# Queries, keys and all gates of a hybrid attention block as Strassen units

## The chip, the core and the metric

The kernel runs on one core of a Trainium2 chip. The core has a matrix engine (TensorE, PE in the profile; its loads of the stationary operand are the row PEld), three engines for elementwise work (VectorE or DVE, ScalarE or ACT, GpSimd or POOL) and SyncE (SP), whose queue issues all transfers of this kernel. The metric is the device time of one execution in microseconds. Before the change the median of three runs is 2264.71 us (2264.17 to 2265.93).

## What is computed

One block of a decoder for 1024 tokens of width 1024, in float32. From one normalised input come, through one wide projection, the queries, keys and values of 12 attention heads of 128, the queries, keys (256 wide), values (512) and output gates of 4 retention heads, and two gates of width 1024:

```python
xn = rmsnorm(x, norm1_g[l])
qa, ka, va, qr, kr, vr, gr, gate_a, gate_b = [xn @ wl[:, bounds[i]:bounds[i + 1]] for i in range(len(IN_SPLITS))]
qa = rmsnorm(qa.reshape(B, S, ATT_HEADS, ATT_HEAD_DIM), q_norm_g[l])
ka = rmsnorm(ka.reshape(B, S, ATT_HEADS, ATT_HEAD_DIM), k_norm_g[l])
...
y = jax.nn.sigmoid(gate_a) * (o_a @ w_proj_a[l]) + jax.nn.sigmoid(gate_b) * (o_r @ w_proj_b[l])
x = x + y @ w_out[l]
```

`o_a` is causal sliding-window attention in three groups of four heads with dilations 1, 4 and 16, whose outputs are mixed by their softmax denominators; `o_r` is chunkwise retention with a group norm and a swish gate. A squared-ReLU MLP follows, which the change does not touch.

## The kernel before

All large products are float32 split in two: a high part rounded to the matrix engine's fast format (`wh`, `xh`), and the rest (`wl`, `xl`). Each product of two blocks is three matmuls (high by high, high by low, low by high), issued by `Pipe.group` (L223). `split` (L319 on ScalarE, L320 on VectorE) makes the two parts. `Weights` loads raw weights through SP (L176) and splits them when the buffer that they go to has been freed by the last product that reads it.

TensorE's order is that of the program text; the other engines' instructions are ordered by a scheduler. `Pipe` counts one slot for each large product (`step`) and lets other work be laid between its terms: `pipe.at(lag, fn)` puts `fn` into the product `lag` slots on, spread evenly over its terms.

The part that the change touches has three stages.

Attention: for each head and each of 8 blocks of 128 tokens, one product gives q, k and v of that head (tokens on partitions, 384 columns, 24 matmuls). q and k are squared and normalised with tokens on partitions (L650, L332, L333, L654), a pair of transposes (`turn_qk`, L660) puts features on partitions, and ScalarE and VectorE write them out in the order of the dilation (L662, L664). Scores (L584), the turn of the probabilities (L597) and their product with the values (L604) are laid into later products of the stage. The groups' outputs go to DRAM and are mixed (`load_heads`, `combine`, `turn_mixed`) while the next heads run, the last ones during retention.

Gates: the first 3 of 8 pairs of gate blocks are plain products of 512 columns, with the sums and differences of the input blocks (`differences`) made alongside.

Strassen units: a unit is a product of 256 output features with all 1024 inputs and tokens, done as seven products (N1 to N7) of 12 matmuls of 512 columns instead of eight, features on partitions. `strassen_order` sets their order, `product` runs one and evicts it: N2 gives one of the four results straight from PSUM, N3 one from `u2` (copied at N6, then a subtraction on VectorE, L402), N7 one from `u3` (a copy on ScalarE, L396, then a subtraction, L397), N4 one from PSUM. `W.free` then lets the next weights into the buffer. Units are 5 gate pairs, 8 retention q and k, and 8 output gates of retention.

Of the kernel before, what the change touches and what calls it, by code (L numbers as in the profile page):

```python
# [17 lines left out]
P = 128  # L18
S = 1024
# [237 lines left out]
def strassen_order(units):  # L257
# [12 lines left out]
def hybrid_block(ctx: ExitStack, tc: tile.TileContext, a: dict, out: bass.AP):  # L270
# [13 lines left out]
    tr = ctx.enter_context(tc.tile_pool(name="tr", bufs=2, space=PSUM))  # L284
    ms = ctx.enter_context(tc.tile_pool(name="ms", bufs=3, space=PSUM))
# [9 lines left out]
    v_d = dram.tile([HEADS, S, DH], F, name="v_d")  # L295

# [25 lines left out]
    half = const.tile([P, 2], F, name="half")  # L322
# [5 lines left out]
    const.tile([P, 224], F, name="rest")  # L328
# [12 lines left out]
    for slot, g in heads:  # L341
        for u in range(4):
            W.add(a["w_att"][g * SLOTS + slot, u])
    for d, bufs in enumerate([(0, 1), (2, 4), (3, 5)]):
        for u, b in enumerate(bufs):
            W.add(a["w_gate"][d, u], b)
    NG, NQ = KT - 3, 2 * RH
    W.add_units("in", [a["w_gate_q"][j] for j in range(NG)] + [a["w_rqk_q"][j] for j in range(NQ)]
                + [a["w_gr_q"][j] for j in range(8)])
# [68 lines left out]
    def dilated(g, b, src, dst):  # L418

        if g == 0:  # L420
            return src, dst[:, b * P:(b + 1) * P]
        r = 4 if g == 1 else 8
        src = src.rearrange("p (i r) -> p r i", r=r)
        if g == 1:
            nb, j = divmod(b, 4)
            return src, dst.rearrange("p (r i) -> p r i", r=r)[:, :, nb * P + 32 * j:nb * P + 32 * j + 32]
        return src, dst.rearrange("p (r i) -> p r i", r=r)[:, :, 16 * b:16 * b + 16]
# [62 lines left out]
    attn = ExitStack()  # L490
    p3 = pool(attn, "p3", 2, "right")
    p2 = pool(attn, "p2", 2, "right")
    cpa = pool(attn, "cpa", 1, "right")
    with ExitStack() as ph:
        cp = pool(ph, "cp", 1)
        first = ExitStack()
        px = pool(first, "px", 2)
        cmb = None

        g1 = cp.tile([P, D], F, name="g1")  # L500
        gq = cpa.tile([P, HEADS], F, name="gq")
        gk = cpa.tile([P, HEADS], F, name="gk")
        dist = cp.tile([P, 2, 2 * P], F, name="dist")
# [55 lines left out]
        pipe.at(0, lambda: W.pump())  # L559
        nc.sync.dma_start(gq, a["q_norm_g"])  # L560
        nc.sync.dma_start(gk, a["k_norm_g"])
        nc.sync.dma_start(dist, a["c_dist"])

        for head, (slot, g) in enumerate(heads):
            h = g * SLOTS + slot
            slope = 2.0 ** (-8.0 * (h + 1) / HEADS)
            us = W.take(4)
            bias = p2.tile([P, 2 * P], F, name="bias")
            qT = p2.tile([P, S], F, name="qT")
            kT = p2.tile([P, S], F, name="kT")  # L570
            V = p2.tile([P, NT, DH], F, name="V")
            Vd = p2.tile([P, NT, DH], F, name="Vd") if g > 0 else V
            acc = p2.tile([P, NT, DH + 2], F, name="acc")

            def attend(g, h, b, bias, qT, kT, V, acc):

                nk = 2 if has_prev(g, b) else 1
                n = nk * P
                k0 = (b + 1 - nk) * P
                st = {}  # L580

                def scores():
                    sp = ms.tile([P, 512], F, name="ms")
                    nc.tensor.matmul(sp[:, :n], qT[:, b * P:(b + 1) * P], kT[:, k0:k0 + n], start=True, stop=True)  # L584
                    s = p3.tile([P, 2 * P], F, name="s")
                    mx = p3.tile([P, 1], F, name="mx")
                    nc.vector.tensor_tensor_reduce(s[:, :n], sp[:, :n], bias[:, 2 * P - n:], op0=OP.add, op1=OP.max,
                                                   scale=1.0, scalar=-3.0e38, accum_out=mx)
                    nc.vector.tensor_scalar(acc[:, b, DH:DH + 1], mx, -1.0, None, op0=OP.mult)
                    st["p"] = p3.tile([P, 2 * P], F, name="pr")  # L590
                    nc.scalar.activation(st["p"][:, :n], s[:, :n], AF.Exp, bias=acc[:, b, DH:DH + 1],
                                         accum_out=acc[:, b, DH + 1:DH + 2])

                def turn():
                    tp = ms.tile([P, 512], F, name="ms")
                    for j in range(nk):
                        nc.tensor.transpose(tp[:, j * P:(j + 1) * P], st["p"][:, j * P:(j + 1) * P], ident)  # L597
                    st["t"] = p3.tile([P, 2 * P], F, name="pT")
                    nc.vector.tensor_copy(st["t"][:, :n], tp[:, :n])

                def values():
                    po = ms.tile([P, 512], F, name="ms")
                    for j in range(nk):
                        nc.tensor.matmul(po[:, :DH], st["t"][:, j * P:(j + 1) * P], V[:, k0 // P + j, :],  # L604
                                         start=(j == 0), stop=(j == nk - 1))
                    nc.scalar.activation(acc[:, b, :DH], po[:, :DH], AF.Copy)
                    if b == NT - 1:
                        store()

                def store():  # L610
# [9 lines left out]
                return scores, turn, values  # L620

            for b in range(NT):
                if b == 1:
                    nc.vector.tensor_scalar(bias, dist[:, 0 if g < 2 else 1, :], -slope * (DIL[g] if g < 2 else 8),
                                            None, op0=OP.mult)
                if head == 0 and b + 2 < NT:
                    norm1(b + 2)
                if head == 1 and b == 4:
                    first.close()
                    cmb = pool(ph, "cmb", 2)  # L630
                if head >= 3:
                    i = head % 3
                    if i < 2 and b == 6:
                        at = load_heads(head // 3 - 1, i, cmb)
                    if i > 0 and b == 1:
                        mixing = combine(head // 3 - 1, i - 1, cmb, at)
                    mix_next()
                if head == 0 and b == 1:
                    nc.vector.tensor_scalar(gq, gq, DH ** -0.5, None, op0=OP.mult)
                ts = slice(b * P, (b + 1) * P)  # L640
                pm = mm.tile([P, 512], F, name="mm")
                o = [(k % 2) * 384 for k in range(KT)]
                w = [W[us[k // 2]] for k in range(KT)]
                ends = {2 * i + 1: (lambda i=i: W.free(us[i])) for i in range(4)} if b == NT - 1 else None
                pipe.step(pm[:, :384], [(*X(k, ts), w[k][0][:, o[k]:o[k] + 384],
                                         w[k][1][:, o[k]:o[k] + 384]) for k in range(KT)], ends)
                ss = p3.tile([P, 4], F, name="ssa")
                junk = p3.tile([P, P], F, name="junk")
                for j in range(2):
                    nc.scalar.activation(junk, pm[:, j * DH:(j + 1) * DH], AF.Square, accum_out=ss[:, j:j + 1])  # L650
                rsqrt(ss[:, 2:4], ss[:, 0:2], 1.0 / DH)
                qk = p3.tile([P, 2, DH], F, name="qk", bufs=3)
                nc.scalar.activation(V[:, b, :], pm[:, 2 * DH:3 * DH], AF.Copy)
                nc.vector.tensor_tensor(qk, pm[:, :2 * DH].rearrange("p (a d) -> p a d", a=2),  # L654
                                        ss[:, 2:4, None].to_broadcast([P, 2, DH]), op=OP.mult)

                def turn_qk(g=g, b=b, h=h, qk=qk, qT=qT, kT=kT):
                    pt = tr.tile([P, 4, P], F, name="tr")
                    for j in range(2):
                        nc.tensor.transpose(pt[:, j, :], qk[:, j, :], ident)  # L660
                    src, dst = dilated(g, b, pt[:, 0, :], qT)
                    nc.scalar.activation(dst, src, AF.Copy, scale=gq[:, h:h + 1])  # L662
                    src, dst = dilated(g, b, pt[:, 1, :], kT)
                    nc.vector.tensor_scalar(dst, src, gk[:, h:h + 1], None, op0=OP.mult)  # L664
# [698 lines left out]
```

## Time and profile before

| | before |
|---|---|
| median of three runs | 2264.71 us |
| profiled execution, its time | 2268.99 us |
| its span, first to last instruction | 2267.2 us |
| TensorE busy, share of the span | 2233.0 us, 98% |
| VectorE, ScalarE, GpSimd busy | 1285.7, 1014.0, 344.3 us |
| attention, first product to first gate product | 10.64 to 521.84 us |
| gates and units, up to retention | 521.84 to about 1001 us |
| mean granted TensorE clock | 0.998 |
| moved by transfers | 294.85 MB, 130 GB/s |

In a row of the order of time stand the start in us, the length in us, the engine, the line, the operation, output and inputs, shapes and a count. Matmuls overlap in the pipeline, so the length of one is longer than the distance to the next. In the grouped rows stand busy time and mean nanoseconds of one, then the idle time of the engine before them. A row of the waits reads: engine, output and line, what it waited for, total us, times, longest.

### The profile page before, as it was taken

The numbers are of one execution on the slowest core, as the hardware profiler recorded it, in microseconds if no ns is written. First come the engines' busy times: TensorE is split into PE (matmuls) and PEld (weight loads), VectorE is DVE, ScalarE is ACT, GpSimd is POOL, SyncE is SP. The second block draws the span as 40 slices with busy tenths as digits, with TensorE's granted clock in tenths as the row PEclk, the third lists the DMA queues.
The fourth block names the chain that finished last, engine by engine and source line by source line (L and its number), as shares of the span: only waits on it lengthen the run. The fifth ranks groups of instructions, "written<-read, shape, count | busy, mean of one in ns | idle before, by whom it ended". The sixth has DMA issues, their size and how long they took to land. (4 is left out here: it accounts for less than half of the span.)

```text
span 2267.2 us, 30458 instructions
## 1 busy us (share of the span) xinstructions
PE 2233.0 (98%) x10868; PEld 1912.0 (84%) x10868; DVE 1285.7 (57%) x2468; ACT 1014.0 (45%) x2294; POOL 344.3 (15%) x372
## 2 busy tenths in 40 slices
PE   8999999999999999999999999999999999899999
PEld 7999999998888888888888878888788888788777
DVE  6444545455544445558676753253855556687874
ACT  5444434345433333345555633112555545654542
POOL 1111111110000000000000000000000000587873
PEclk9999999999999999999999999999999999999999
DMA  4313232323233333363433385554345556645432
GB/s 148 98 52 105 65 91 85 94 85 99 82 109 106 110 109 111 113 186 117 122 117 97 121 267 183 155 184 153 107 127 151 151 152 199 218 153 179 169 129 102
DMA packets 227146, 294.85 MB, mean 130 GB/s; under 512 B 14129, under 2 KB 157873, under 8 KB 226994
## 3 DMA queue, kind: packets, MB, share of 16 engines
q1 hardware_dynamic: 226994, 292.91, 41.1%
q8 instruction: 85, 1.39, 0.3%
q14 instruction: 67, 0.55, 0.1%
HBM read 200.48 MB, written 92.37 MB: 129 GB/s over the span
## 5 line engine op out<-in xcount | busy, mean ns | idle before, releaser
L320 DVE TENSOR_TENSOR wl<-raw,wh 128x1024 fp32r<-128x1024 f32 (+2 forms) x274 | 300.4, 1099 | 398.0 <-ACT wh L319 396.9
L223 PE MATMUL mm<-wh,xh 128*128 128x384 f32 (+1 forms) x1226 | 482.0, 393 | 0.6 <-DVE Y L1203 0.5
L223 PE MATMUL mm<-wh,xl 128*128 128x384 f32 (+1 forms) x1226 | 438.8, 358 | 2.2 <-DVE xl L320 2.2
L223 PE MATMUL mm<-wl,xh 128*128 128x384 f32 (+1 forms) x1226 | 437.7, 357 | 0.0
L319 ACT ACTIVATE wh<-raw 128x1024 fp32r<-128x1024 f32 (+2 forms) x274 | 260.0, 951 | 358.2 <-PE ms L223 102.2
L223 PE MATMUL mm<-xl,wh 128*128 128x512 f32 x848 | 309.3, 389 | 1.7 <-DVE xl L320 1.7
L223 PE MATMUL mm<-xh,wh 128*128 128x512 f32 x848 | 309.7, 390 | 0.9 <-ACT ms L388 0.9
L223 PE MATMUL mm<-xh,wl 128*128 128x512 f32 x720 | 280.1, 389 | 0.0
L223 PEld LDWEIGHTS mm<-wh,xl 128*128 128x128 f32 x1226 | 230.9, 188 | 22.2 <-DVE xl L320 3.0
L223 PEld LDWEIGHTS mm<-wh,xh 128*128 128x128 f32 x1226 | 231.8, 189 | 20.0 <-DVE Y L1203 1.3
L223 PEld LDWEIGHTS mm<-wl,xh 128*128 128x128 f32 x1226 | 232.7, 190 | 16.6
L223 PE MATMUL ms<-xh,wh 128*128 128x512 f32 x604 | 239.3, 396 | 5.0 <-DVE s L941 3.5
L223 PE MATMUL ms<-xl,wh 128*128 128x512 f32 x604 | 235.8, 390 | 0.7 <-DVE xl L320 0.7
L223 PE MATMUL ms<-xh,wl 128*128 128x512 f32 x604 | 235.9, 391 | 0.0
L223 PEld LDWEIGHTS mm<-xl,wh 128*128 128x128 f32 x848 | 159.2, 188 | 34.9 <-DVE xl L320 2.1
L223 PEld LDWEIGHTS mm<-xh,wh 128*128 128x128 f32 x848 | 159.2, 188 | 34.2 <-ACT ms L388 1.3
L223 PEld LDWEIGHTS mm<-xh,wl 128*128 128x128 f32 x720 | 135.1, 188 | 28.1
L853 POOL TENSOR_TENSOR st<-st,half 128x1 f32<-128x1 f32 x32 | 25.8, 808 | 765.3 <-DVE st L852 765.3
L223 PEld LDWEIGHTS ms<-xh,wh 128*128 128x128 f32 x604 | 113.9, 189 | 31.2 <-issue 2.3
L223 PEld LDWEIGHTS ms<-xh,wl 128*128 128x128 f32 x604 | 113.7, 188 | 23.9
L223 PEld LDWEIGHTS ms<-xl,wh 128*128 128x128 f32 x604 | 113.9, 189 | 23.5 <-DVE xl L320 1.0
L333 POOL TENSOR_TENSOR ssa<-ssa,half 128x2 f32<-128x2 f32 x96 | 66.5, 693 | 427.9 <-DVE ssa L332 411.2
(296 smaller groups left out, 3605.1 us busy)
## 6 DMA issues: line engine op xcount, KB each, us to landing
raw<-in_w_att SPq DMA_DIRECT2D x48, 384.0 KB, 3.9
raw<-in_w_up SPq DMA_DIRECT2D x32, 512.0 KB, 3.9
h_d<-s SPq DMA_DIRECT2D x64, 256.0 KB, 4.5
raw<-in_w_down SPq DMA_DIRECT2D x32, 512.0 KB, 4.1
xh<-h_d SPq DMA_DIRECT2D x11, 896.0 KB, 4.5
xl<-h_d SPq DMA_DIRECT2D x10, 896.0 KB, 4.6
r<-h_d SPq DMA_DIRECT2D x10, 896.0 KB, 5.6
sg_d<-sg SPq DMA_DIRECT2D x32, 256.0 KB, 2.0
```

The source lines that it names most:

```text
L223: self.nc.tensor.matmul(ps, x, y, start=start, stop=stop, skip_group_check=not first)
L319: nc.scalar.activation(dst_h, src, AF.Copy)
L320: nc.vector.tensor_tensor(dst_l, src, dst_h.bitcast(F), op=OP.subtract)
L333: nc.gpsimd.tensor_tensor(dst, dst, half[:, :w], op=OP.pow)
L853: nc.gpsimd.tensor_tensor(st[:, 9:10], st[:, 8:9], half[:, 0:1], op=OP.pow)
```

## The change

The values of all heads become plain products ahead of everything, four heads at once (512 columns, 24 products of 24 matmuls), written to DRAM. The q and k of each head become one Strassen unit, and all 8 gate pairs become units. The units number 36 instead of 21, in a new order in which the next unit starts one unit ahead instead of two. With features on partitions no transposes of q and k are needed. The sum of squares over features then runs across partitions: a matmul with the squares as stationary operand and a column of ones. Norms are raised on GpSimd, turned, written to DRAM and read back broadcast over partitions; q and k go through DRAM as well, and a head's attention starts when its pieces have been read back and multiplied. Attention of a head takes 11 slots, 8 of them with scores, laid between unit products from the 24th slot on; all mixing follows after the last head, so none is left for retention. The N4 operand takes the place of one input block, which is kept in DRAM and read back at the end. `u2` and `u3` get one buffer instead of two; three PSUM buffers instead of two serve the inserted work, two instead of three the `ms` tiles.

```diff
+    if near:
+        order = [(0, "N1"), (0, "N2")]
+        for j in range(units):
+            for d, name in ((0, "N6"), (0, "N5"), (1, "N1"), (0, "N7"), (1, "N2"), (0, "N3"), (0, "N4")):
+                if j + d < units:
+                    order.append((j + d, name))
+        return order
...
-    tr = ctx.enter_context(tc.tile_pool(name="tr", bufs=2, space=PSUM))
-    ms = ctx.enter_context(tc.tile_pool(name="ms", bufs=3, space=PSUM))
+    banks = ExitStack()
+    tr = banks.enter_context(tc.tile_pool(name="tr0", bufs=3, space=PSUM))
+    ms = banks.enter_context(tc.tile_pool(name="ms0", bufs=2, space=PSUM))
...
-    NG, NQ = KT - 3, 2 * RH
+    NG, NQ, NH = KT, 2 * RH, HEADS
...
+        def head_piece(i, f, cs, src):
...
+            sq = ap.tile([P, 512], F, name="sq")
+            nc.scalar.activation(sq, src, AF.Square)
+            sg = src
+            if src.space == PSUM:
+                sg = sgp.tile([P, 512], F, name="sg")
+                nc.scalar.activation(sg, src, AF.Copy)
+            nc.sync.dma_start(qk_d[h, f, :, cs], sg)
...
+            def sums():
+                ps = tr.tile([P, 512], F, name="tr")
+                for c in range(4):
+                    nc.tensor.matmul(ps[:, c:c + 1], sq[:, c * P:(c + 1) * P], one, start=True, stop=True)
+                nc.vector.tensor_scalar(rs[:, f, t:t + 4], ps[:, :4], 1.0 / DH, EPS, op0=OP.mult, op1=OP.add)
+                norms[i][1] += 1
+                if norms[i][1] == 4:
+                    flat = rs.rearrange("p f t -> p (f t)")
+                    nc.gpsimd.tensor_tensor(flat, flat, half, op=OP.pow)
+                    pipe.at(2, turn_norms)
...
+            pipe.at(0, sums)
...
+        def norm_piece(i, n):
...
+            dst, raw, rb = dilated(g, hf, state[i]["qk"[f]], raw, rb)
+            nc.vector.scalar_tensor_tensor(dst, raw, (gk if f else gq)[:, h:h + 1], rb, op0=OP.mult, op1=OP.mult)
+
+        def open_head(i):
...
+            for n in range(4):
+                norm_piece(i, n)
+                if n < 2:
+                    load_piece(i, n + 2)
...
+            pipe.at(0, scores)
+            pipe.at(2, turn)
+            pipe.at(3, values)
+
+        PACE = NT + 3
+        starts = [pipe.slot + 24 + PACE * i for i in range(HEADS)]
...
-                pm = mm.tile([P, 512], F, name="mm")
-                o = [(k % 2) * 384 for k in range(KT)]
...
-                        nc.tensor.transpose(pt[:, j, :], qk[:, j, :], ident)
...
-        for j, name in strassen_order(NIN):
+        for j, name in strassen_order(NIN, near=True):
+            between()
```

How the instructions stand now is set by these tables and by the scheduler. First TensorE, in a product of the attention stage before (`mm` of 384 columns, a score matmul L584 and the pair of transposes L660 laid in):

```order
L584 MATMUL ms_2703<-kT_1675,qT_1674 128x256
L223 MATMUL mm_2679<-wh4_2531,xh_93 128x384
L223 MATMUL mm_2679<-wl4_2532,xh_93 128x384
L223 MATMUL mm_2679<-wh4_2531,xl_94 128x384
L223 MATMUL mm_2679<-wh5_2547,xh_93 128x384
L223 MATMUL mm_2679<-wl5_2548,xh_93 128x384
L223 MATMUL mm_2679<-wh5_2547,xl_94 128x384
L660 MATMUL tr_2717<-ident_101,qk_2596 128x128 x2
```

The pair stands behind the last but one term of a product of 24 matmuls. Now the product N2 of a unit, which follows N7 of the unit before; L754 are the values, L743 the turn, L653 the four sums over N7's squares, L730 the scores:

```order
L754 MATMUL tr_1883<-V0_1735,pT_1850 128x128
L223 MATMUL mm_1815<-xh_96,wh0_1521 128x512
L223 MATMUL mm_1815<-xl_97,wh0_1521 128x512
L223 MATMUL mm_1815<-xh_96,wl0_1522 128x512
L743 MATMUL tr_1889<-ident_104,pr_1832 128x128 x2
L223 MATMUL mm_1815<-xh_96,wh0_1521 128x512
L223 MATMUL mm_1815<-xl_97,wh0_1521 128x512
L223 MATMUL mm_1815<-xh_96,wl0_1522 128x512
L653 MATMUL tr_1897<-one_1211,sq_1868 128x1 x4
L223 MATMUL mm_1815<-xh_96,wh0_1521 128x512
L223 MATMUL mm_1815<-xl_97,wh0_1521 128x512
L223 MATMUL mm_1815<-xh_96,wl0_1522 128x512
```

The transposes are gone; the sums stand behind the ninth of the twelve matmuls of N2. Second, ScalarE around the end of N7, in a unit before (`wh5` is the split of weights that N7 frees, `u3` the copy of N7's result):

```order
L319 ACTIVATE wh5_7805<-raw0_7561 128x1024
L396 ACTIVATE u3_7801<-ms_7539 128x512
L750 ACTIVATE sg_7829<-mm_7774 128x512
L319 ACTIVATE wh4_6606<-raw2_7685 128x512
L750 ACTIVATE sg_7844<-ms_7539 128x512
```

And now (L642 are the squares, L737 the exponentials, L756 the copies of the attention's output):

```order
L330 ACTIVATE wh5_1871<-raw0_1493 128x1024
L737 ACTIVATE pr_1857,md_1699<-pr_1857,md_1699 128x128
L404 ACTIVATE u3_1865<-ms_1640 128x512
L756 ACTIVATE acc_1882<-tr_1883 128x128
L642 ACTIVATE sq_1868<-u3_1865 128x512
L330 ACTIVATE wh0_1919<-raw1_1877 128x1024
L642 ACTIVATE sq_1914<-mm_1815 128x512
L646 ACTIVATE sg_1916<-mm_1815 128x512
```

The split still goes ahead of the copy; the square of `u3` and the square of the next N2 are new, with work of attention between. Third, VectorE at the same place now:

```order
L734 ISA pr_1857,mx_1858<-tr_1855,bias_1698 128x128
L734 ISA mx_1858 128x1
L736 TENSOR_SCALAR md_1699<-mx_1858 128x1
L331 TENSOR_TENSOR wl5_1872<-raw0_1493,wh5_1871 128x1024
L405 TENSOR_TENSOR u3_1865<-u3_1865,mm_1792 128x512
L745 COPY pT_1892<-tr_1889 128x256
L654 TENSOR_SCALAR rs_1686<-tr_1897 128x4
```

The subtraction from `u3` stands behind the low half of the split, and the reading of the sums (L654) behind both.

More of the change, by code (lines that the diff above doesn't have):

```diff
@@ L560, in hybrid_block @@
+    with ExitStack() as ph:
+        pu = pool(ph, "pu0", 1)
+        attn = ExitStack()
+        ap = pool(attn, "ap", 2)
+        gq = ap.tile([P, HEADS], F, name="gq", bufs=1)
+        gk = ap.tile([P, HEADS], F, name="gk", bufs=1)
         nc.sync.dma_start(gq, a["q_norm_g"])
         nc.sync.dma_start(gk, a["k_norm_g"])
-        nc.sync.dma_start(dist, a["c_dist"])
-        for head, (slot, g) in enumerate(heads):
-            h = g * SLOTS + slot
[L566 to L610, printed above, removed]
@@ L618, in store @@
                         nc.sync.dma_start(acc_d[:, h, :].rearrange("(p r) e -> p r e", r=8), acc)
[L620 to L640, printed above, removed]
-                pm = mm.tile([P, 512], F, name="mm")
-                o = [(k % 2) * 384 for k in range(KT)]
[L643 to L664, printed above, removed]
-                s1, s2, s3 = attend(g, h, b, bias, qT, kT, Vd, acc)
-                lag = 2 if g == 0 else 9
-                pipe.at(lag + 2, s3)
-                pipe.at(lag + 1, s2)
-                pipe.at(lag, s1)
-                pipe.at(1, turn_qk)
@@ new lines, in hybrid_block, with between @@
+        mixes = starts[-1] + PACE + 4
+        cmb, at = None, {}
+        def between():
+            nonlocal mixing, cmb
+            now = pipe.slot
+            for i, start in enumerate(starts):
+                if now == start - 6:
+                    load_piece(i, 0)
+                    load_piece(i, 1)
+                if now == start - 3:
+                    open_head(i)
+                if now == start - 2:
+                    load_values(i, 0)
+                if now == start + 1:
+                    load_values(i, 1)
+                if start <= now < start + NT:
+                    attend(i, now - start)
+            if now == mixes - 1:
+                attn.close()
+                cmb = pool(ph, "cmb", 2)
+            n, m = divmod(now - mixes, 9)
+            if 0 <= n < 2 * SLOTS and m == 0:
+                at[n] = load_heads(n // 2, n % 2, cmb)
+            n, m = divmod(now - mixes - 5, 9)
+            if 0 <= n < 2 * SLOTS and m == 0:
+                mixing = combine(n // 2, n % 2, cmb, at[n])
+            mix_next()
@@ L770, in hybrid_block @@
                 start = values(first, slice(0, P), False)
+            if (j, name) == (NIN - 1, "N4"):
+                for i in range(2):
+                    nc.sync.dma_start(XS[0, 1][i].bitcast(F), x_d[i])
+        assert not mixing and not any(f >= pipe.slot for f in pipe.due), (pipe.slot, mixes, pipe.due.keys())
         W.more = None
     gst.close()
+    banks.close()
+    tr = ctx.enter_context(tc.tile_pool(name="tr", bufs=2, space=PSUM))
+    ms = ctx.enter_context(tc.tile_pool(name="ms", bufs=3, space=PSUM))
     ret = ExitStack()
@@ L1296, in _constants @@
     far = np.where((d >= 0) & (d <= P) & (k >= P) & (d % 2 == 0), d, BIG)
-    dist = np.stack([near, far], 1).astype(np.float32)
+    bias = []
+    for h in range(HEADS):
+        g = h // SLOTS
+        scale = -(2.0 ** (-8.0 * (h + 1) / HEADS)) * (DIL[g] if g < 2 else 8)
+        bias.append((near if g < 2 else far).astype(np.float32) * np.float32(scale))
     mask = np.zeros((P, RH, P), np.float64)
```

281 lines of the change are left out of this document (174 added, 107 removed).

## The prediction

> **What bounds the kernel now.** I read the busy times first, then what TensorE waited for, then its order of time. The page and the two lists of TensorE's waits (the first 530 us, then up to 996 us, which is the end of the part that the change rewrites):
>
> ```profile
> span 2267.2 us, 30458 instructions
> PE 2233.0 (98%) x10868; PEld 1912.0 (84%) x10868; DVE 1285.7 (57%) x2468; ACT 1014.0 (45%) x2294; POOL 344.3 (15%) x372
> ...
> PE mm L223 <- DVE xl L320: 2.2, 2, 1.7
> PE ms L584 <- DVE pT L599: 0.9, 1, 0.9
> ...
> PE ms L597 <- ACT sg L689: 0.4, 1, 0.4
> PE ms L604 <- ACT sg L689: 0.2, 1, 0.2
> ```
>
> After its first matmul TensorE waits under 5 us in this whole part. So the part lasts as long as TensorE has instructions for, and the change is priced in TensorE's time; whatever VectorE, ScalarE and the transfers do costs only where TensorE has to wait for it. The profiled execution took 2268.99 us, 1.8 us more than its span; the median of the runs is 2264.71 us, and I subtract from that, since a difference of instructions is the same in both.
>
> A busy figure of matmuls overlaps (390 ns each), so I take start-to-start times from the order of time:
>
> ```profile
> 299.81 0.33 PE L223 MATMUL mm<-wh,xh 128*128 128x384 f32 x1
> ...
> 302.75 0.34 PE L223 MATMUL mm<-wh,xl 128*128 128x384 f32 x1
> 302.94 0.38 PE L660 MATMUL tr<-ident,qk 128*128 128x128 f32 x2
> 303.07 0.42 PE L223 MATMUL mm<-wh,xh 128*128 128x384 f32 x1
> 303.33 0.34 PE L223 MATMUL mm<-wl,xh 128*128 128x384 f32 x1
> ...
> 991.80 0.39 PE L223 MATMUL mm<-wh,xl 128*128 128x512 f32 x1
> 997.92 0.39 PE L223 MATMUL ms<-xh,wl 128*128 128x512 f32 x1
> ```
>
> From 299.81 to 302.75 are 17 steps of 384 columns: 0.173 us each. From 991.80 to 997.92 are 27 steps of 512 columns: 0.2267 us. The pair of transposes stretches two steps from 0.346 to 0.58 us, so it costs 0.234 us.
>
> **Products: removed and added.** The attention projections are 12 heads x 8 blocks x 8 k x 3 = 2304 matmuls of 384 columns: 398.6 us. The three plain gate groups are 3 x 4 x 8 x 3 = 288 of 512: 65.3 us. The transposes of q and k, 96 pairs: 22.5 us. Removed: 486.4 us. Added: values plain, 3 x 8 x 8 x 3 = 576 of 512; 12 units of q and k and 3 more gate units, each 7 products of 12: 1260 of 512. That is 1836 x 0.2267 = 416.2 us. Scores, turns of the probabilities, values and the mixing are moved, with the same count. Net so far: -70.2 us.
>
> **The column of ones.** Each of 48 results (12 heads, q and k, two halves) now passes through four matmuls of one column whose stationary operand is a 128x128 float32 block of squares. No such matmul is in the trace. The nearest rows are the four passes of a float32 product with 128 columns (two products; the profile shows two passes for each), and the weight loads around such insertions:
>
> ```profile
> 525.71 0.40 PE L223 MATMUL ms<-xh,wl 128*128 128x512 f32 x1
> 525.94 0.61 PE L604 MATMUL ms<-V,pT 128*128 128x128 f32 x4
> 526.30 0.47 PE L223 MATMUL ms<-xh,wh 128*128 128x512 f32 x1
> 526.62 0.39 PE L223 MATMUL ms<-xl,wh 128*128 128x512 f32 x1
> ...
> 511.83 0.58 PEld L604 LDWEIGHTS ms<-V,pT 128*128 128x128 f32 x4
> ...
> 515.74 0.19 PEld L223 LDWEIGHTS mm<-wh,xh 128*128 128x128 f32 x1
> 515.85 0.19 PEld L223 LDWEIGHTS mm<-wl,xh 128*128 128x128 f32 x1
> ```
>
> The four passes cost 0.91 - 0.453 = 0.457 us, 0.114 each. With one column almost nothing streams, so the weight load must set the pace. Loads follow each other at 0.11 us where no long matmul lies between (515.74, 515.85), and at (0.58 - 0.19) / 3 = 0.13 within the four. Four matmuls make eight passes: 8 x 0.114 = 0.91 us, and 48 of these 43.8 us. Bounds: if half of each load ran under the one before, 22 us; if each took its whole 0.19 us, 8 x 0.19 x 48 = 73 us. I take 43.8, since the load spacing is the row closest to it.
>
> The Trainium skill ("TensorE: Matmul & The Clock Gate", section "Back-to-back issue gap") prices an isolated matmul of 1 to 64 columns at an issue floor of about 25 ns; by that the eight passes would take 0.2 us, 48 of them an estimated 10 us, and the kernel 34 us less than I say. The load spacing of 0.11 us speaks against it here, since every pass loads its own weights.
>
> Turning the 16 norms of a head costs half a pair of transposes, 12 x 0.117 = 1.4 us. The sums themselves are read by VectorE and raised on GpSimd, both of which have room: VectorE was busy 250 of 511 us in the attention part and 184 of 401 in the unit part:
>
> ```profile
> 10.64:521.84 511.20, 507.88 (x3137) 496.14 (x3136) 250.17 (x892) 235.58 (x927) 69.86 (x102) 1.00 0.29 88
> ...
> 595.00:996.00 401.00, 401.00 (x1770) 331.78 (x1769) 184.43 (x229) 147.53 (x212) 0.00 (x0) 1.00 0.34 112
> ```
>
> Squares on ScalarE (48 x 0.63) and the four multiplications of a head on VectorE (0.68 each, as the 512-wide L867) replace the 192 squares with their accumulators, the 96 qk multiplications and the 192 scaled evictions. They cost nothing as long as no product of TensorE waits. Without that cover each would cost its own length.
>
> Net without waits: -70.2 + 43.8 + 1.4 = -25.0 us.
>
> **The new waits.** The sums stand in the very next product, after nine of its twelve matmuls in most slots (the order of TensorE in the part on the change): 9 x 0.2267 = 2.04 us, plus the values and the turn ahead of them (0.35 to 0.69), so about 2.5 us after the product ends. Three of the four results make that. N2 and N4 are squared straight from PSUM behind one weight split (0.97 + 0.63 = 1.6 us). N3 needs a VectorE subtraction first (0.16 + 0.68 + 0.63 = 1.5 us). N7 does not. The same chain in the trace of before, where N7 of a unit ended and the next product started at 731.36:
>
> ```profile
> 731.36 0.39 PE L223 MATMUL mm<-xh,wh 128*128 128x512 f32 x1
> ...
> 731.33 1.06 ACT L319 ACTIVATE wh<-raw 128x1024 fp32r<-128x1024 f32 x1 [1.38 <-PE ms L223]
> 732.30 0.58 ACT L396 ACTIVATE u<-ms 128x512 f32<-128x512 f32 x1
> ...
> 732.43 1.23 DVE L320 TENSOR_TENSOR wl<-raw,wh 128x1024 fp32r<-128x1024 f32 x1 [1.70 <-ACT wh L319]
> 733.57 0.68 DVE L397 TENSOR_TENSOR u<-u,mm 128x512 f32<-128x512 f32 x1
> ...
> L746 ACT ACTIVATE sg<-u 128x512 f32<-128x512 f32 x13 | 8.2, 632 | 20.2 <-DVE u L402 12.7 <-DVE u L397 7.5
> ```
>
> The split of the freed weights goes ahead of the copy on ScalarE and ahead of the subtraction on VectorE, so the difference is ready 734.25 - 731.36 = 2.9 us after the product; a square of 0.63 us (as the sigmoid in L746) puts it at 3.5. The new order keeps both splits ahead, so TensorE would wait 3.5 - 2.5 = 1.0 us. Where the slot has no scores, the sums stand at the product's end and the next split (1.06 us) goes ahead of the square: 0.16 + 0.97 + 0.63 = 1.8 us. With three such slots in eleven the mean is 1.2 us, and 12 heads give 14.4 us. Behind the waiting sums stand the product's last matmuls, the scores and all later products: nothing of it is made up, since TensorE is the bound.
>
> Opening a head makes VectorE wait for two 256 KB loads that SP issues only after its first two multiplications:
>
> ```profile
> s<-sg_d SPq DMA_DIRECT2D x32, 256.0 KB, 3.3
> rqk_d<-u SPq DMA_DIRECT2D x16, 256.0 KB, 3.8
> ```
>
> From the last scores of the head before: about 4 us to the first two multiplications, 0.7 for two issues, 3.3 to land, 0.7 for the last: 9 us. The new head's scores are due four products later, 4 x 2.72 plus insertions, about 14: covered. But the copy of the last turned block stands behind it on VectorE, done at about 9.4 and due at about 10. I charge 0.4 us a head, 5 us (0 to 25). The store of u2, now in one buffer, lands about 0.9 + 0.35 + 3.8 = 5 us after N3, and the next u2 copy comes at 5.4 or later: nothing, and 4 us more of cover before N7. At the start the 2.2 us wait for xl shrinks, as the first products are a third longer: -1 us.
>
> Sum: -25.0 + 14.4 + 5 - 1 = -6.6 us, 2258.1 us.
>
> **Rivals.** (a) The waits stay hidden, or the one-column passes are cheaper than their loads suggest. For it: TensorE waited almost nowhere in either old part, and a square put ahead of the split would be in time. Against it: the order has the split ahead. No waits: 2264.7 - 26 = 2239; with passes at half a load too, 2217.
> (b) Slower: all four sums of a unit wait, not N7's alone. ScalarE then has the splits, the evictions, the squares and the exponentials of attention in one strict order, and each square is late by whatever stands ahead. For it: the margins of the other three are only 0.9 us, while one exponential takes 0.4 to 0.5 and one split 1.06. Against it: both engines were about half idle. If the other 36 sums wait x on average, the time is 2258.1 + 36x; it is slower than before by the measurable amount from x = 0.31 us. At x = 0.7 it is 2283.
> (c) Loads of float32 squares cost their whole 0.19 us: 73 instead of 43.8 us, 2287.
>
> **How the numbers follow.** This kernel's runs tell about 0.2% from no change, 4.5 us: below 2260.2 is faster, above 2269.2 slower. My case, 0.42, with a range of its own from 2248 to 2268: within it 0.25 faster, 0.13 same, 0.04 slower. Rival (a) 0.25, all faster. Rivals (b) 0.24 and (c) 0.09: 0.02 the same, the rest slower. That makes 0.50 faster, 0.15 same, 0.35 slower. The range takes in (a) with hidden waits and (b) and (c) at their prices: 2234 to 2287.
>
> **What would show it.** The matmuls L653 should hold their product up by 0.9 us per four (half of that: (a); 1.5: (c)). The list of TensorE's waits should show the first of L653 waiting for ScalarE's square of u3 a dozen times, near 1.2 us. If the squares of mm, u2 and ms stand there too, it is (b). The copies pT should show a few short waits near the opening of heads; the unit products should still start every 0.2267 us. The prediction is wrong if a wait that I took as covered, the loads at a head's opening above all, comes to several us for each head.

## The result and the profile after

The changed kernel takes 2303.49 us (median of four runs, 2296.13 to 2309.46), the kernel before 2265.32 us beside it: 1.0164 times as long, with a 95% interval of 1.0133 to 1.0196. It is slower by 38 us; 2258 us was predicted, with 2287 as the upper end of the range. The head of the page of the changed kernel's profiled execution:

```profile
span 2302.3 us, 29056 instructions
...
PE 2236.7 (97%) x10316; PEld 1834.5 (80%) x10316; DVE 1341.6 (58%) x2385; ACT 1034.6 (45%) x1910; POOL 315.1 (14%) x288
```

TensorE shows 552 matmuls fewer than before (10868), and the span is 35.1 us longer. The rewritten part holds the loss: the first matmul of retention starts at 1046.51 us instead of 1002.91, 43.6 us later, and what follows it is 8.5 us shorter than before. TensorE's waits in this part, of which there had been less than 5 us (us in total, times, longest):

```profile
PE tr L653 <- ACT sq L642: 15.6, 12, 2.0
PE tr L481 <- DVE oa L475: 10.2, 7, 4.0
PE tr L754 <- DVE pT L745: 4.8, 5, 1.9
...
PE mm L223 <- DVE u L405: 3.3, 4, 1.3
...
PE mm L223 <- ACT ms L396: 1.4, 1, 1.4
PE tr L663 <- POOL rs L658: 1.3, 1, 1.3
```

The first row is the one that was predicted: twelve waits of the sums (L653) for the square of N7. The second was not: the transposes of a mixed block (L481) wait for VectorE's mixing. The rows together have 36.6 us. And there is a cost that no list of waits shows. The table by stretches (from and to, length, busy time of PE, PEld, DVE, ACT and POOL with their counts, then the granted TensorE clock, the DMA share and GB/s):

```profile
150.00:450.00 300.00, 280.73 (x1409) 231.51 (x1407) 140.93 (x310) 117.23 (x248) 28.71 (x9) 0.95 0.42 130
450.00:840.00 390.00, 382.21 (x1870) 314.32 (x1869) 222.06 (x521) 185.84 (x378) 9.84 (x3) 1.00 0.53 154
840.00:1000.00 160.00, 149.32 (x634) 119.87 (x633) 102.48 (x236) 72.90 (x103) 0.00 (x0) 0.96 0.42 131
```

The clock was 0.95 in the stage of q and k, and 0.96 in the stage of the mixing: 0.05 x 300 + 0.04 x 160 = 21 us of TensorE's time. Over slices of 30 us, where the rounding matters less, it is 20.7 us. The kernel before had 1.00 there.

How the two belong together is seen in the order of time around the first N7 (start, length, engine, line, operation, and in brackets the idle time before it and what ended it):

```profile
172.52 0.58 ACT L404 ACTIVATE u<-ms 128x512 f32<-128x512 f32 x1
172.65 1.23 DVE L331 TENSOR_TENSOR wl<-raw,wh 128x1024 fp32r<-128x1024 f32 x1 [6.28 <-ACT wh L330]
...
173.79 0.68 DVE L405 TENSOR_TENSOR u<-u,mm 128x512 f32<-128x512 f32 x1
...
174.51 0.63 ACT L642 ACTIVATE sq<-u 128x512 f32<-128x512 f32 x1 [1.40 <-DVE u L405]
175.19 1.05 PE L653 MATMUL tr<-one,sq 128*128 128x1 f32 x8 [1.46 <-ACT sq L642]
176.10 0.48 PE L223 MATMUL mm<-xh,wh 128*128 128x512 f32 x1
...
177.61 0.63 PE L223 MATMUL mm<-xh,wh 128*128 128x512 f32 x1
...
178.03 0.63 PE L223 MATMUL mm<-xl,wh 128*128 128x512 f32 x1
...
178.46 0.63 PE L223 MATMUL mm<-xh,wl 128*128 128x512 f32 x1
```

The copy of N7 is there early; the subtraction stands behind a weight split of 1.23 us on VectorE, the square behind the subtraction, and TensorE waits 1.46 us. About 2.4 us after it works again, its matmuls start every 0.42 us instead of every 0.23, until the next sums at 180.17: half the clock. (The trace also records the granted clock with its times: 0.5 from 177.52 us, for 3.41 us.) So the wait is paid once as a wait, and a second time afterwards.

The mixing, later on:

```profile
898.70 0.49 PE L481 MATMUL tr<-ident,oa 128*128 128x128 f32 x3
...
900.96 1.23 DVE L331 TENSOR_TENSOR wl<-raw,wh 128x1024 fp32r<-128x1024 f32 x1 [1.12 <-ACT wh L330]
...
902.42 0.74 DVE L475 SCALAR_TENSOR_TENSOR oa<-at,w,oa 128x128 f32<-128x128 f32 x2
...
903.22 0.47 PE L481 MATMUL tr<-ident,oa 128*128 128x128 f32 x1 [4.03 <-DVE oa L475]
...
904.34 0.63 PE L223 MATMUL mm<-xh,wl 128*128 128x512 f32 x1
904.77 0.63 PE L223 MATMUL mm<-xh,wh 128*128 128x512 f32 x1
```

Three of the four transposes run; the fourth needs the last mixing step, which stands on VectorE behind the sums and splits of the weights for the next units. They are due one product after that step, and a product of a unit gives VectorE only 2.72 us. TensorE waits 4.03 us, and half the clock follows.

The theory to be tested: the loss is TensorE's waits for work that is laid too close ahead of its consumer, plus the clock that falls after such waits. The main rivals: the clock falls for a reason of its own, such as the one-column passes; or the waits only move on when a consumer is put later.

### The profile page after: what moved, and what is told of

It reads as the page before. It is cut to its first block, busy times and chain, and to the rows that moved or that the text cites. A ratio compares the mean times of both kernels' runs of the same rounds, so it can differ in the third digit from the quotient of the medians.

```text
span 2302.3 us, 29056 instructions
## 1 busy us (share of the span) xinstructions
PE 2236.7 (97%) x10316; PEld 1834.5 (80%) x10316; DVE 1341.6 (58%) x2385; ACT 1034.6 (45%) x1910; POOL 315.1 (14%) x288
## 5 line engine op out<-in xcount | busy, mean ns | idle before, releaser
L331 DVE TENSOR_TENSOR wl<-raw,wh 128x1024 fp32r<-128x1024 f32 (+1 forms) x292 | 327.6, 1123 | 376.6 <-ACT wh L330 371.4
L223 PE MATMUL mm<-xh,wh 128*128 128x512 f32 x1088 | 431.1, 415 | 5.3 <-DVE u L405 3.3
L330 ACT ACTIVATE wh<-raw 128x1024 fp32r<-128x1024 f32 (+1 forms) x292 | 283.0, 970 | 331.9 <-PE ms L223 145.1
L223 PE MATMUL mm<-xh,wl 128*128 128x512 f32 x960 | 380.3, 396 | 0.0
L223 PE MATMUL mm<-wh,xh 128*128 128x512 f32 x458 | 185.7, 405 | 0.6 <-DVE Y L1277 0.4
L223 PE MATMUL mm<-wh,xl 128*128 128x512 f32 x458 | 179.7, 392 | 0.0
L223 PE MATMUL mm<-wl,xh 128*128 128x512 f32 x458 | 178.5, 390 | 0.0
L223 PEld LDWEIGHTS mm<-wh,xl 128*128 128x128 f32 x458 | 85.9, 188 | 18.8
L223 PEld LDWEIGHTS mm<-wh,xh 128*128 128x128 f32 x458 | 86.1, 188 | 17.4 <-DVE Y L1277 1.3
L223 PEld LDWEIGHTS mm<-wl,xh 128*128 128x128 f32 x458 | 86.4, 189 | 15.7
```

Of the source, the lines that this page charges most:

```text
L223: self.nc.tensor.matmul(ps, x, y, start=start, stop=stop, skip_group_check=not first)
L330: nc.scalar.activation(dst_h, src, AF.Copy)
L331: nc.vector.tensor_tensor(dst_l, src, dst_h.bitcast(F), op=OP.subtract)
```

## Experiments

Every time below is a median with the kernel before measured beside it; its medians were 2263.80 to 2265.64 us.

**The sums one product later.**

```diff
-            pipe.at(0, sums)
+            pipe.at(1, sums)
```

> Edit: the four one-column sums of every result go one product later; nothing else is changed. Theory A (TensorE's waits for the squares of N7, 20.1 us in twelve waits, and the granted clock that falls after such pauses, 13.8 us of TensorE's time lost between 150 and 450 us): both go, the list of TensorE's waits shows no L653 behind ScalarE's square, the clock column shows no slice under 1.00 before 840 us, and the time falls by about 34 us to 2270 us (2264 to 2278). Rival 1 (the clock falls for another reason, such as the one-column passes themselves, and the waits alone go): 2283 us, with the clock's dips still there. Rival 2 (the next product is as full, and the wait only moves to another consumer): 2298 to 2305 us.

Measured: 2269.29 us (2267.97 to 2272.16), 34.2 us less, where 34 were expected. The waits for N7's square are gone from the list, where they had 15.6 us (the expectation had counted 20.1). Beside that the copies pT are waited for 3.6 us less and u3 3.4 us more, so the close agreement of the sum is in part luck. The same table of stretches for this kernel:

```profile
150.00:450.00 300.00, 294.79 (x1567) 246.54 (x1566) 156.51 (x352) 130.09 (x282) 32.61 (x10) 1.00 0.45 143
...
840.00:1000.00 160.00, 151.65 (x647) 122.03 (x646) 97.10 (x205) 69.18 (x97) 0.00 (x0) 0.97 0.40 131
```

The clock is 1.00 up to 450 us with every one-column pass still there, and stays low in the mixing, which was not touched. The passes alone don't lower it.

**Work in place of the wait.** The sums stay where the change put them.

```diff
                 ps = tr.tile([P, 512], F, name="tr")
+                if f and t:
+                    x = XS[0, 0][0]
+                    for _ in range(6):
+                        nc.tensor.matmul(ps, x[:, 0, :P], x[:, 0, :], start=True, stop=True)
```

> Edit: in the changed kernel, six plain products of 512 columns (1.36 us), whose results nobody reads, are put right ahead of the sums of N7, twelve times, so that TensorE works where it would wait. The sums start when they started before, or a little later where the wait was shorter than the filling (some 2 to 4 us in all). Theory A (a pause of TensorE brings the clock down afterwards): the dips of the clock before 450 us, 13.8 us, mostly go although work is added, so 2303 + 3 - 12 = about 2294 us (2290 to 2297), and the part after 840 us keeps its dips. Rival 1 (the clock falls for another reason): the dips stay, 2306 us.

Measured: 2290.35 us (2288.11 to 2301.64). Twelve times 1.36 us of work that nobody needs make the kernel 13 us faster than the changed one by the medians; three of its four executions took 2288 to 2292 us, and one took 2301.64 at a mean granted clock of 0.992 instead of 0.996. The first stretch of the profiled one:

```profile
150.00:450.00 300.00, 293.09 (x1536) 243.20 (x1535) 147.67 (x333) 122.17 (x264) 31.97 (x10) 1.00 0.43 133
```

The squares are as late as they were; only TensorE no longer stands still, and the clock is 1.00. So it is the pause that brings the clock down, and in this stage it was worth some 14 us. The waits for the squares fell from 15.6 to 2.4 us, which pays for most of the added work (16.3 us).

**The turning of mixed blocks one product later.**

```diff
-                pipe.at(1, mixing.pop())
+                pipe.at(2, mixing.pop())
```

> Edit: the four transposes that turn a mixed block (L481) go two products after the last step of the mixing instead of one; the sums stay where they are. Theory A: the 12.5 us that these transposes cost over their old price, and the 6.9 us of granted clock lost between 840 and 990 us, go: 2303 - 19 = 2284 us (2280 to 2290), and the waits of L481 for VectorE's oa are gone from the list. Rival 1 (the clock falls for another reason): 2291 us. Rival 2 (VectorE is so far behind in this part that the next reader of it waits instead): 2300 us or more.

Measured: 2290.92 us (2283.16 to 2292.86), 12.6 us less instead of 19. The waits of this kernel:

```profile
PE tr L653 <- ACT sq L642: 15.2, 12, 2.0
PE mm L223 <- DVE u L405: 7.9, 5, 2.9
...
PE tr L481 <- DVE oa L475: 2.3, 2, 1.3
```

L481's waits fall from 10.2 to 2.3 us, but the unit products' own waits for VectorE's subtraction of u3 (L405) rise from 3.3 to 7.9: a part of the gain moves on, as the second rival said. The time is that of the first rival (2291 us, the clock stays low), but its mechanism is not seen: between 840 and 1000 us the clock rose from 0.96 to 0.99.

**Sums, mixing and values later, all three.** The values of attention go four products after the scores, not three.

```diff
-            pipe.at(3, values)
+            pipe.at(4, values)
```

> Edit: the sums one product later, the transposes of the mixing one product later, and the values of attention four instead of three products after the scores. Theory A: waits of 20 + 12 + 8 us and 20.7 us of granted clock go, 2303 - 61 = 2242 us (2236 to 2252), faster than the kernel before by about 20 us, with 1.00 in every slice of the clock up to 990 us. Rival 1 (waits go, the clock stays): 2263 us. Rival 2 (the waits move on to other readers of VectorE and ScalarE): 2275 us or more.

Measured: 2262.79 us (2260.61 to 2263.75); ratio to the kernel before 0.9991 (0.9982 to 1.0001). The theory had said 2242. It was incomplete. The first rival had said 2263 for waits that go and a clock that stays low; its number came out, but not its reason, for the clock is 1.00 in all three stretches of the table. TensorE and VectorE at the longest of the waits that are left, each from its own order of time, TensorE first:

```profile
807.14 0.39 PE L223 MATMUL mm<-xh,wl 128*128 128x512 f32 x1
809.80 0.50 PE L223 MATMUL mm<-xh,wh 128*128 128x512 f32 x1 [2.27 <-DVE u L405]
```

```profile
807.67 1.22 DVE L331 TENSOR_TENSOR wl<-raw,wh 128x1024 fp32r<-128x1024 f32 x1
808.80 0.34 DVE L475 SCALAR_TENSOR_TENSOR oa<-at,w,oa 128x128 f32<-128x128 f32 x1
809.06 0.68 DVE L405 TENSOR_TENSOR u<-u,mm 128x512 f32<-128x512 f32 x1
```

The product that waits is N3. It goes on in the bank in which N5 stands, and the subtraction of u3 still has to read N5 there. In the order of the kernel before, N4 stood between; the change put N3 first. That leaves u3 one product of 2.72 us instead of two. Seven such waits make 9.8 us in this kernel, and its order of time has 13 more delays of 0.2 to 0.3 us between products, 2.9 us, that the list of waits doesn't name.

**N4 ahead of N3 again.** On top of the three. u2 gets its second buffer back; the room is taken from the second buffer of the bias and from 864 bytes of padding among the constants.

```diff
-    ... (1, "N2"), (0, "N3"), (0, "N4")):
+    ... (1, "N2"), (0, "N4"), (0, "N3")):
...
-    const.tile([P, 216], F, name="rest")
...
-            u["u2"] = pu().tile([P, 512], F, name="u2")
+            u["u2"] = pu().tile([P, 512], F, name="u2", bufs=bufs)
```

> Edit, on top of all three later places: the unit's last two products change places (N4, then N3, as in the kernel before), so that N3, which goes on in the bank that the subtraction of u3 reads, has one product more of cover; for that u2 gets two buffers and the bias one. Theory (the rest of what was missing is N3 waiting for u3: seven waits of 9.8 us, a delay of 0.2 us in another 20 units, 4.4 us, and 1 us of clock): 2263 - 15 = 2248 us (2243 to 2254), faster than the kernel before by 0.6%, and L223 no longer waits for VectorE's u of L405. Rival (the bank of N3 is now read last, and the next unit's N5 waits for u2's subtraction instead): 2260 us or more, with waits for u of L410 in the list.

Measured: 2259.85 us (2257.90 to 2265.22), ratio 0.9977 (0.9968 to 0.9986). Neither expectation held. The waits for u3 were gone and none for u2 had come, and the part ended at 989.56 us instead of 1001.48; but everything behind it took 1273.8 us instead of 1259.7 (in a profiled execution of 2265.22 us, the longest of eleven). From about 1420 us on its matmuls started every 0.232 us instead of every 0.2267, with a granted clock of 1.00. The slower pace had begun earlier: between 840 and 980 us they started every 0.2308 us, where they had started every 0.2273. No instruction behind the part had changed; the padding had.

**The padding kept.** The same kernel with the small tiles (gammas, ones, norms) put into the padding, so that the weights and operands lie where they lay before.

> The kernel with N4 ahead of N3 again, but the 864 bytes of padding among the constants, which had been given up there to make room, are kept: small tiles (gammas, the ones, the norms) take part of the padding's place, so that every weight and operand tile lies at the address that it has in the changed kernel. Theory (the 14 us that came back behind the unit part there, a matmul pitch of 0.232 instead of 0.2267 us from about 1420 us on, come from the addresses of the moving operands): the unit part ends at 990 us as there, the rest takes 1260 us as with all three later places, together 2250 us (2245 to 2254), and the pitch is 0.2267 to the end. Rival (it is the chip's clock in a kernel that pauses less): 2260 us again.

Measured: 2240.30 us (2239.52 to 2241.05), ratio 0.9896 (0.9881 to 0.9911). 19.6 us came from the addresses of the tiles alone. The time is 10 us under the 2250 expected, and 8.5 of them lie in the rewritten part, which ends at 981.01 us instead of 989.56: the slower pace had cost time there too. Two more kernels have the same instructions and only less padding:

> The kernel with N4 ahead of N3 and unchanged addresses, with 32 bytes of padding less: every weight and operand tile lies 32 bytes lower (the first weight tile at byte 17088 of its partition, a multiple of 64, where it lay at 17120). No instruction changes. Theory of the addresses, if a multiple of 64 is what costs: the pitch of 0.232 us returns and with it some 20 us: 2260 us (2252 to 2264). If only a multiple of 128 costs: 2240 us. Rival (addresses don't matter; the 20 us between the two kernels came from elsewhere): 2240 us here and with 96 bytes.

> The same with 96 bytes of padding less (the first weight tile at 17024, a multiple of 128, as it was a multiple of 128 in the kernel that lost 20 us). Theory of the addresses: 2260 us (2252 to 2264). Rival: 2240 us.

Measured: 2258.22 us (2255.95 to 2260.76) and 2259.38 us (2257.72 to 2260.61). A stretch of plain products behind the part, of the kernel with the padding kept and of the one with 32 bytes less:

```profile
1400.00:1560.00 160.00, 160.00 (x707) 132.54 (x706) 68.19 (x92) 33.22 (x52) 0.55 (x1) 1.00 0.51 168
```

```profile
1400.00:1560.00 160.00, 160.00 (x694) 129.77 (x693) 61.16 (x83) 31.01 (x48) 0.00 (x0) 1.00 0.49 159
```

Both are without a gap and at the full clock (TensorE works on the same instructions in the same order), but the second gets 694 matmuls into the 160 us where the first gets 707: 1.9% fewer. A shift by 32 bytes does it as a shift by 864 did. So addresses matter; that a multiple of 64 bytes is what costs fits all three shifted kernels, but only these places were tried.

**N7's sums early, or the other three.** In the kernel with the padding kept, the sums of N7 alone, or of the other three results alone, go back into the very next product.

```diff
-            pipe.at(1, sums)
+            pipe.at(0 if f and t else 1, sums)
```

> The kernel with N4 ahead of N3 and unchanged addresses, with one thing put back: the sums of N7 alone (a quarter of the 48) go into the very next product, as in the changed kernel. Theory (N7 alone is late, and its pauses bring the clock down): 20 us of waits and up to 14 us of clock return: 2250 + 27 = 2277 us (2266 to 2286), with some twelve waits of L653's matmuls for ScalarE's square, mean 1.7 us. Rival (the other three results are late too, so that N7 is a part of it): 2260 us or less.

> The complement: the sums of N2, N3 and N4 go into the very next product, those of N7 one later. Theory (these three are in time there): as without it, 2250 us (2246 to 2256), with less than 2 us of waits for the squares. Rival (their margin of about 0.9 us is too small): 36 sums wait 0.3 us and more, 2261 us or above.

Measured: 2268.49 us (2264.18 to 2273.57) with N7 early, 28.2 us more, and 2249.17 us (2245.09 to 2251.13) with the others early, 8.9 us more. The row of the squares in the first of these kernels, and in the second:

```profile
PE tr L654 <- ACT sq L643: 16.8, 12, 3.4
```

```profile
PE tr L654 <- ACT sq L643: 2.5, 4, 1.2
```

N7 has most of it: 16.8 us of waits, and the rest is about what the clock takes, whose records stand at 0.5 for 23.9 us in this part (11.9 us lost). The other three have four waits, 2.5 us, and one stretch of 3.41 us at half clock (1.7 us lost), so they are nearly in time; the 8.9 us that they cost fall between the expectations, and not all of them are explained.

**One pass in place of two.** On top of N4 first: the squares are rounded to fp32r, and two columns of ones take the place of one.

```diff
-            sq = ap.tile([P, 512], F, name="sq")
+            sq = ap.tile([P, 512], R, name="sq")
...
-                    nc.tensor.matmul(ps[:, c:c + 1], sq[:, c * P:(c + 1) * P], one, start=True, stop=True)
+                    nc.tensor.matmul(ps[:, 2 * c:2 * c + 2], sq[:, c * P:(c + 1) * P], one, start=True, stop=True)
```

> [...] Theory (the sums are paced by their weight loads, 0.114 us each): 4 x 0.114 = 0.46 us instead of 0.91 per four sums, 48 x 0.45 = 22 us less: 2226 us (2221 to 2232). Rival 1 (an fp32r load of squares is no shorter than both passes of float32): 2248 us. Rival 2 (nearly free once the second pass is gone, about 0.1 us per four): 2209 us.

> The kernel with single-pass sums, with the padding kept in the same way. Theory of the addresses: 968 + 1260 = 2228 us (2223 to 2233), the fastest of all here, 1.6% under the kernel before. Rival (the clock): 2239 us.

Measured: 2238.76 us (2235.42 to 2241.09), 21.1 us less than without it, and with the padding kept 2219.29 us (2217.28 to 2222.10), 21.0 us less. The 22 us of the theory came. The times themselves lie outside the ranges that were expected: the first is 12.8 us above its 2226, which was counted without the slower pace, and the second 8.7 us below its 2228, which took the slower pace to cost nothing in the rewritten part. The sums in the changed kernel, where nothing waits, and in the single-pass kernel:

```profile
161.54 0.40 PE L223 MATMUL ms<-xh,wl 128*128 128x512 f32 x1
161.77 0.95 PE L653 MATMUL tr<-one,sq 128*128 128x1 f32 x8
...
162.90 0.40 PE L223 MATMUL ms<-xl,wh 128*128 128x512 f32 x1
```

```profile
196.51 0.39 PE L223 MATMUL ms<-xh,wl 128*128 128x512 f32 x1
196.74 0.50 PE L654 MATMUL tr<-one,sq 128*128 128x2 f32 x4
...
197.42 0.39 PE L223 MATMUL ms<-xl,wh 128*128 128x512 f32 x1
```

Less two steps of 0.2267 us, eight passes cost 1.36 - 0.453 = 0.91 us and four cost 0.91 - 0.453 = 0.46: 0.114 us for each pass with its weight load, in both. Passes and loads were halved together, so these runs don't separate the load from the pass. The kernel with single passes and the padding kept is the fastest: 0.9804 times the kernel before (0.9790 to 0.9819).

## Why the prediction was wrong

**Right: TensorE's own work.** The step "Net without waits" gave -25 us, and 2239 us as the time with every wait hidden (rival a). The kernel in which they are hidden takes 2240.30. The agreement to a microsecond has some luck in it: behind the rewritten part 6.6 us were saved that nobody had predicted, and inside it the matmuls between 160 and 840 us started every 0.2294 us on average, not every 0.2267 (about 2200 matmuls, 6 us). So the part itself became 21.9 us shorter, not 26.

**Right: the price of the column of ones.** 0.91 us for four sums was predicted from the spacing of weight loads, and 0.91 was measured; halving the passes and their loads halved it. The issue floor that the Trainium skill ("TensorE: Matmul & The Clock Gate", section "Back-to-back issue gap") would have given for so few columns is not what these passes cost. Rival (c), loads at their full 0.19 us, falls.

**Right in place, mechanism and size: the wait for N7.** Twelve waits of the sums for the square of u3 were predicted at 1.2 us each, 14.4 us; there were twelve, 15.6 us, for the reason given: the weight split stands ahead of the subtraction. What failed is the tacit rule that a wait costs its own length: put back alone into the clean kernel, these waits of 16.8 us cost 28.2.

**Wrong: no term for the clock.** The sum had every matmul at 0.2267 us, waits or not. 20.7 us went to half clock behind pauses. Filling the pauses with useless work showed where it came from. This is the largest missing term.

**Wrong: the mixing at nothing.** "Scores, turns of the probabilities, values and the mixing are moved, with the same count." The count was the same, the distance was not: one product between the last mixing step and the transposes was enough before, when six of the eight blocks were turned in the attention stage, where a product takes 24 x 0.173 = 4.15 us, and two in retention. Among the units, at 2.72 us a product and behind their sums and splits of weights, it was not. 10.2 us of waits; with one product more 2.3 are left. The prediction named what hides the squares and the norms, but never asked it for the work that it called moved.

**Wrong: the new order of N3 and N4.** The step on u2 counted what the order does for u2's store and found 4 us more of cover. It didn't ask what else N3 touches: the bank that u3's subtraction still reads. That showed as 3.3 us of waits in the changed kernel, and as 9.8 us of waits and 13 small delays once the longer waits elsewhere were gone; with N4 ahead and nothing shifted, the time fell by 22.5 us (2262.79 to 2240.30). A part of that, which wasn't separated, may be that u2 has two buffers again.

**Right in size, in part by luck: the opening of a head** at 5 us. The copies pT were waited for in five places, 4.8 us. But the four multiplications, taken at 0.68 us each from L867, took 1.13 us each (the median of L690), and two of the longest waits of N7, 2.0 and 1.9 us, belong to them too, since on VectorE they stand ahead of the subtraction there.

**Rival (b)**, slower because all four sums of a unit wait, had the right sign and the wrong place: the other three results waited 2.5 us together where they were early alone.

By the profiled spans the forecast is missed by 41.7 us (35.1 longer, not 6.6 shorter): 50.2 in the rewritten part, less 8.5 behind it. Of the 50.2, the clock has 20.7, the mixing 10.2, u3 3.3 and the longer waits of N7 1.2. Some 9 more are the matmul pitch (6 us), a wait of 1.4 us at the first unit and one of 1.3 us of the norms for GpSimd. Of the last 6, some 5 lie in how a wait is counted (an estimate): a row counts from the end of the last matmul, which is 0.39 us long at a pitch of 0.2267, so each of the thirty waits costs about 0.16 us more than its row has. Why the pitch is 0.2294 in this part, at the old addresses and largely at full clock, stays open.

## What to carry to other kernels

When a kernel is bound by TensorE, price a pause at its length plus what follows at half clock; here that made 28 us of 17, and moving a consumer one product later, or even filling the hole with useless work, paid. When work is moved to a place with a faster beat, count every lag again in microseconds, not in slots, and for each reordered product ask which bank it writes and who still reads it. And when memory is re-divided, keep the large tiles where they were, or measure the shift by itself before judging the edit.

## What the hardware showed that was not expected

A pause of TensorE of 0.9 to 2 us is enough to bring the clock to half, but not each time. In the changed kernel, five of nine waits of the sums between 0.9 and 2.1 us were followed by such a stretch, and all three waits of the mixing over 2 us. By the clock records of the trace the stretch began 0.4 to 2.3 us after these pauses of the sums, and in two of the three of the mixing before the pause was over. Of the nine stretches of the rewritten part seven last 3.41 us, one 6.83 and one 10.24. The first wait of N7, 1.46 us in three kernels, was followed by one in two of them and not in the third. The Trainium skill ("TensorE: Matmul & The Clock Gate", Part 1 on the HAM clock gate) tells of a free-running window of activity of about 3.4 us. The traces agree: within each trace all such stretches start on one grid of 3.41 us, wherever the pause lies.

Cut along this grid, the traces of the changed kernel and of its twelve variants also tell which pauses count. Between 100 and 1000 us they have 3395 windows of 3.41 us at full clock. Take as idle the time without a matmul and that of the one-column passes: the next window stood at half clock after all 25 with more than 1.87 us idle, after three of the eight with 1.80 to 1.87 us, and after none of the others. So a pause that falls across the border of two windows can pass unpunished, and the sums beside a pause count with it: 0.90 us of waiting next to them was enough in three kernels, and 1.82 us without them in one window was not. That the passes count as idle is read from this fit alone.

The Trainium skill ("TensorE: Matmul & The Clock Gate", section "HAM oscillation") gives the rule of no idle gaps over about 3.4 us. Most of the pauses here were shorter and cost clock all the same, so for this kernel the rule is too generous.

The start address of the tiles changes the pace of the 512-column matmuls by 2%: 707 against 694 matmuls in 160 us, with 32 bytes of shift and no other difference, and 18 to 20 us of the whole in the three shifted kernels. Which operand's address it is was not tried. The Trainium skill ("SBUF — State Buffer", section "Operand start alignment") says which start addresses are legal and that this is not about speed; about speed these runs are all there is.
